# Loading V in 8 KB runs, eight heads at a time, in a cross-covariance attention kernel

One Trainium2 chip, one core. The metric is the device time of one execution in microseconds (us), median of several runs. The span of a profiled run is the part of it from the first to the last instruction. A run is called slow when it takes over 1.5% longer than the fastest run of the same kernel, else fast. Medians below count all runs; ratios, and every comparison of two kernels, use fast runs alone.

## The reference

Per head (8 x 12 heads, 512 rows n, 64 columns d), all in fp32:

```python
Q_norm = Q / norm(Q, over n);  K_norm = K / norm(K, over n)
attn = softmax(Q_norm^T K_norm, over the last axis)      # 64 x 64
out  = V attn                                            # 512 x 64
```

## The kernel before

Heads go in 24 units of four. A unit of Q, K or V is 512 KB on 128 partitions: 32 partitions per head, 16 rows (4 KB) in each. Gram matrices are taken from bf16 casts of Q and K; V is cast to bf16, transposed by TensorE into one bank of PSUM, and copied from there (evicted) by ScalarE into vt, whose slices are the weights of the last matmul. What the change and the argument touch:

```python
def load_v(u):
    vf[u] = vp.tile([128, R * D], F32, name="vf")                 # R = 16, D = 64
    nc.sync.dma_start(out=vf[u], in_=Vf[u])

def cast_v(u):                                                    # half ScalarE, half VectorE
    w = vb[u] = vbp.tile([128, R // 2, 2 * D], BF16, name="vb")
    for half, copy in ((slice(0, TP), nc.scalar.copy), (slice(TP, None), nc.vector.tensor_copy)):
        copy(w[:, half], vf[u].rearrange("p (t d) -> p t d", d=2 * D)[:, half])

def vtrans(u):
    ps = ps_v.tile([128, R // 2, 128], BF16, name="vps")
    for t in range(R // 2):
        nc.tensor.transpose(ps[:, t, :], vb[u][:, t, :], identb)
    w = vt[u] = vtp.tile([128, TP, 128, 2], BF16, name="vt")
    nc.scalar.copy(w.rearrange("p t c a -> p a t c"),             # L148, "the eviction"
                   ps.rearrange("p (a t) c -> p a t c", a=2))

def outs(u, copies=(nc.scalar.copy, nc.scalar.copy)):             # ... cut
    nc.tensor.matmul(po[...], vt[u][:, t, NV * h:NV * (h + 1), :].rearrange("p c a -> p (c a)"), ...)
    copies[g](s[:, g], po)

for s in range(U):                                                # ... cut
    on(load_qk, s + LOAD_AHEAD)
    while nv < min(U, n1 + 4):                                    # n1: units done by this step
        load_v(nv); nv += 1
    # stores, then cast_v, cast_q(s+1), norms, grams(s), ..., outs, vtrans
# closing phase: the last units' V by fp32 transposes (vtrans_f32), without a cast
```

In vt the two values with the same column c lie side by side (a), so consecutive c are 4 bytes apart. The eviction runs along c: it writes bf16 at a step of 4 bytes. The weights need (c a) at one even step, and the order of a in c decides the order of output rows, so that each partition stores 2 KB in one run.

Of the kernel before, what the change touches and what calls it, by code (L numbers as in the profile page):

```python
# [8 lines left out]
F32 = mybir.dt.float32  # L9
BF16 = mybir.dt.bfloat16  # L10
# [4 lines left out]
D = 64  # L15
HU = 4
NV = 32
R = 16
SV = 2
MV = 64  # L20
TP = 4
# [3 lines left out]
def kernel(  # L25
# [7 lines left out]
    nc = tc.nc  # L33
    B, H, N, _ = Q.shape
    assert N == NV * R and Q.shape[3] == D
    U = B * H // HU

    Qf, Kf, Vf = (x.rearrange("b h n d -> (b h n d)").rearrange("(u p f) -> u p f", p=128, f=R * D) for x in (Q, K, V))
    Of = out.rearrange("b h n d -> (b h n d)").rearrange("(u s p f) -> u p s f", s=SV, p=128, f=TP * 2 * D)

    ctx.enter_context(tc.manual_schedule())

    const = ctx.enter_context(tc.tile_pool(name="const", bufs=1))
    qp = ctx.enter_context(tc.tile_pool(name="qp", bufs=5))
    vp = ctx.enter_context(tc.tile_pool(name="vp", bufs=6))
    vbp = ctx.enter_context(tc.tile_pool(name="vbp", bufs=4))
    qkp = ctx.enter_context(tc.tile_pool(name="qkp", bufs=4))
    vtp = ctx.enter_context(tc.tile_pool(name="vtp", bufs=3))
    sop = ctx.enter_context(tc.tile_pool(name="sop", bufs=10))
# [2 lines left out]
    ps_v = ctx.enter_context(tc.tile_pool(name="ps_v", bufs=1, space=bass.MemoryType.PSUM))  # L52
# [5 lines left out]
    def outs_by(s):  # L58

        return max(0, (s - 2) * 9 // 10)  # L60


    qf, kf, vf, vb, qkb, nsq, rq, kqs, sl, ex, vt, so, kq = ({} for _ in range(13))

    def load_qk(u):
        qf[u] = qp.tile([128, R, D], F32, name="qf")
        kf[u] = qp.tile([128, R, D], F32, name="kf")
        nc.sync.dma_start(out=qf[u].rearrange("p t d -> p (t d)"), in_=Qf[u])
        nc.sync.dma_start(out=kf[u].rearrange("p t d -> p (t d)"), in_=Kf[u])

    def load_v(u):
        vf[u] = vp.tile([128, R * D], F32, name="vf")
        nc.sync.dma_start(out=vf[u], in_=Vf[u])

    def store(u, g=slice(0, SV)):
        nc.sync.dma_start(out=Of[u][:, g], in_=so[u][:, g].rearrange("p s t d -> p s (t d)"))

    def cast_q(u):
        qkb[u] = qkp.tile([128, R, 2 * D], BF16, name="qkb")
        nc.vector.tensor_copy(qkb[u][:, :, 0:D], qf[u])  # L80
# [1 line left out]
    def cast_k(u):  # L82
        nc.vector.tensor_copy(qkb[u][:, :, D:], kf[u])  # L83

    def cast_v(u):
        w = vb[u] = vbp.tile([128, R // 2, 2 * D], BF16, name="vb")
        for half, copy in ((slice(0, TP), nc.scalar.copy), (slice(TP, None), nc.vector.tensor_copy)):
            copy(w[:, half], vf[u].rearrange("p (t d) -> p t d", d=2 * D)[:, half])  # L88

    def grams(u):  # L90

# [29 lines left out]
    def logits(u):  # L121
        for h in range(HU):
            nc.tensor.transpose(lg[:, h, :], kqs[u][D:, h, :], ident[D:, D:])  # L123

    def scale_q(u):
        s = sl[u] = small.tile([D, HU, D], F32, name="sl")
        nc.vector.tensor_tensor(out=s, in0=lg, in1=rq[u][0:D, :, None].to_broadcast([D, HU, D]), op=ALU.mult)  # L127

    def exps(u):
        e = ex[u] = small.tile([D, HU, D], F32, name="ex")  # L130
        nc.scalar.activation(e, sl[u], AF.Exp)  # L131

    def normalise(u):
        s = small.tile([D, HU], F32, name="esum")
        nc.vector.reduce_sum(out=s, in_=ex[u], axis=AX.X)  # L135
        ri = small.tile([D, HU], F32, name="rinv")
        nc.vector.reciprocal(ri, s)
        a = abuf[u % len(abuf)]
        nc.vector.tensor_tensor(out=a[0:D, :, 0, :], in0=ex[u], in1=ri[:, :, None].to_broadcast([D, HU, D]), op=ALU.mult)  # L139

    def vtrans(u):

        ps = ps_v.tile([128, R // 2, 128], BF16, name="vps")
        for t in range(R // 2):
            nc.tensor.transpose(ps[:, t, :], vb[u][:, t, :], identb)  # L145

        w = vt[u] = vtp.tile([128, TP, 128, 2], BF16, name="vt")
        nc.scalar.copy(w.rearrange("p t c a -> p a t c"), ps.rearrange("p (a t) c -> p a t c", a=2))  # L148

    def vtrans_f32(u):  # L150

        w = vt[u] = vtp.tile([128, TP, 128, 2], BF16, name="vt")
        for i in range(2):
            half = slice(i * TP // 2, (i + 1) * TP // 2)
            ps = ps_t.tile([128, TP // 2, 128, 2], F32, name="vps32")
            for t in range(TP // 2):
                for a in range(2):
                    c = (a * TP + i * TP // 2 + t) * 2 * D
                    nc.tensor.transpose(ps[:, t, :, a], vf[u][:, c:c + 2 * D], ident)  # L159
            both[i](w[:, half], ps)  # L160

    def doubled(u):

        a = abuf[u % len(abuf)]
        nc.tensor.matmul(dup[D:], identb[0:D, 0:D], a[0:D, :, 0, :], tile_position=(0, D))  # L165
        nc.scalar.copy(a[D:, :, 1, :], dup[D:])  # L166

    def outs(u, copies=(nc.scalar.copy, nc.scalar.copy)):
        s = so[u] = sop.tile([128, SV, TP, 2 * D], F32, name="so")
        a = abuf[u % len(abuf)]  # L170
        for g in range(SV):
            po = ps_o.tile([128, TP, 2 * D], F32, name="po")
            for t in range(TP):
                for x in range(2):
                    h = 2 * g + x
                    nc.tensor.matmul(  # L176
                        po[MV * x:MV * (x + 1), t, :], vt[u][:, t, NV * h:NV * (h + 1), :].rearrange("p c a -> p (c a)"),
                        a[:, h].rearrange("p a d -> p (a d)"), tile_position=(0, MV * x),
                    )
            copies[g](s[:, g], po)  # L180
# [11 lines left out]
    ident = const.tile([128, 128], F32, name="ident")  # L192
    make_identity(nc, ident)
    identb = const.tile([128, 128], BF16, name="identb")
# [4 lines left out]
    for i in range(12):  # L199
        a = const.tile([128, HU, 2, D], BF16, name=f"ab{i}")  # L200
# [3 lines left out]
    def on(f, u):  # L204
        if 0 <= u < U:
            f(u)

    on(cast_q, 0)
    on(cast_k, 0)
    on(load_v, 0)  # L210
    on(load_v, 1)
    nv, nst, nt = 2, 0, 0
    for s in range(U):
        n0, n1 = outs_by(s - 1), outs_by(s)
        on(load_qk, s + LOAD_AHEAD)
        while nv < min(U, n1 + 4):
            load_v(nv)
            nv += 1
        while nst < n1 - 3:
            store(nst)  # L220
            nst += 1
        new = range(nt, n1 + 1) if s >= 1 else ()
        for v in new:
            cast_v(v)
        on(cast_q, s + 1)
        on(normalise, s - 2)
        on(grams, s)
        on(norms, s)
        on(keep_kq, s)
        on(scale_k, s)  # L230
        on(logits, s - 1)
        on(scale_q, s - 1)
        on(exps, s - 1)
        on(cast_k, s + 1)
        for v in range(n0, n1):
            outs(v)
        on(doubled, s - 2)
        for v in new:
            vtrans(v)
            nt = v + 1  # L240
# [3 lines left out]
    ps_t = ctx.enter_context(tc.tile_pool(name="ps_t", bufs=4, space=bass.MemoryType.PSUM))  # L244
    both = (nc.scalar.copy, nc.vector.tensor_copy)

    for i, u in enumerate(range(n1, U)):
        on(load_v, u + 4)
        store(u - 3)
        if i == 0:  # L250
            normalise(last - 1)
        if i == 2:
            scale_q(last)
            exps(last)
        if i == 3:
            normalise(last)
        on(vtrans_f32, u + 1)
        if i == 1:
            doubled(last - 1)
        if i == 3:  # L260
            doubled(last)
        outs(u, both)
        if i == 1:
            logits(last)
    for u in range(U - 3, last):
        store(u)
    for g in range(SV):
        store(last, slice(g, g + 1))
# [29 lines left out]
```

## Time and profile before

| | before |
|---|---|
| time, median of 3 runs | 132.05 us (131.41 to 132.57) |
| span of the profiled run | 129.3 us |
| busy: DMA engines (dynamic queue) | 98.1% |
| busy: VectorE, ScalarE, TensorE, GpSimd | 76%, 69%, 66%, 52% |
| eviction of vt, L148 | 19 x 1303 ns |
| ScalarE, cast of V | 19 x 619 ns |

How to read it: the DMA engines are the one resource near 100%; the prediction below shows the lines (columns of the timeline: start, duration, engine, line, operation, out<-in, count). These are ScalarE's instructions for one unit, from the timeline of the kernel before (columns: start, duration, engine, line, operation, out<-in, count):

```profile
82.40 1.31 ACT L148 COPY vt<-vps 128x1024 bf16<-128x1024 bf16 x1
83.56 0.63 ACT L88 CAST vb<-vf 128x512 bf16<-128x512 f32 x1
84.41 0.37 ACT L100 COPY kq<-gram 64x256 f32<-64x256 f32 x1 [0.22 <-DVE nsq L107]
84.80 0.42 ACT L131 ACTIVATE ex<-sl 64x256 f32<-64x256 f32 x1
85.24 1.07 ACT L180 COPY so<-po 128x512 f32<-128x512 f32 x2
86.34 0.37 ACT L166 CAST ab<-lgdup 64x256 bf16<-64x256 f32 x1
86.73 1.30 ACT L148 COPY vt<-vps 128x1024 bf16<-128x1024 bf16 x1
```

From one eviction to the next it is 4.33 us here, against 5.06 us of transfers per unit (three loads and a store at the pace of the loop).

### The profile page before, as it was taken

To read this page: it belongs to the slowest core of one execution; us is meant where nothing else is said; L and a number is where in the kernel's file an instruction comes from. 1 tells how busy PE (TensorE), PEld (TensorE's weight loads), DVE (VectorE), ACT (ScalarE), POOL (GpSimd) and SP (SyncE) were. 2 spreads that over 40 slices of the span, in tenths; PEclk is the share of its full clock that TensorE was granted. 3 is DMA by queue.
4 is the path that set the end of the run, shared out by engine and by line. 5 is a ranking of instruction groups with operands and counts; after the bars stand their busy time and mean duration, and the time that the engine had idled before them with its cause. 6 is when DMAs were issued, how large, how long until landed. Compare 5 with 4: busy or idle time off the path is not lost.

```text
span 129.3 us, 5436 instructions
## 1 busy us (share of the span) xinstructions
PE 85.7 (66%) x2232; PEld 65.9 (51%) x2232; DVE 98.3 (76%) x366; ACT 88.7 (69%) x158; POOL 67.6 (52%) x68
## 2 busy tenths in 40 slices
PE   0034878689667976829975776674997567697700
PEld 0033666557455754617854564452875455575500
DVE  0776787987996799839799998695699768698610
ACT  3003342548998899985795799996979997976700
POOL 7924567773785377525387768375075356500000
PEclk9999999999998699995599999997579999999995
DMA  4999999999999999999999999999999999999991
GB/s 137 402 416 418 414 403 406 412 404 402 416 403 406 416 408 412 412 408 414 404 413 411 421 406 416 409 412 411 412 411 406 416 404 413 409 411 390 348 376 68
DMA packets 16936, 50.67 MB, mean 392 GB/s; under 512 B 1552, under 2 KB 1552, under 8 KB 16912
## 3 DMA queue, kind: packets, MB, share of 16 engines
q1 hardware_dynamic: 16912, 50.34, 98.1%
q8 instruction: 17, 0.28, 0.8%
q14 instruction: 7, 0.06, 0.1%
HBM read 37.75 MB, written 12.58 MB: 389 GB/s over the span
## 4 chain that ended last, share of the span: by engine, by line
PE 25%; DMA 22%; ACT 19%; DVE 11%; issue 10%; POOL 6%; SPq 1%; ACTq 0%; POOLq 0%; DVEq 0%
DMA qf<-in_Q_dram 22%; PE gram L95 8%; ACT vt L148 7%; PE po L176 6%; ACT so L180 6%; DVE scr L107 5%; POOL rq L112 5%; PE vps L145 4%; PE vps L159 3%; ACT kq L100 3%; ACT ab L166 2%; PE lgdup L123 2%; ACT ex L131 2%; PE lgdup L165 2%; POOL kqs L117 1%
## 5 line engine op out<-in xcount | busy, mean ns | idle before, releaser
L112 POOL TENSOR_TENSOR rq<-nsq,mhalf 128x4 f32<-128x4 f32 x24 | 45.9, 1913 | 42.5 <-DVE nsq L107 31.7
L95 PE MATMUL gram<-qkb 32*128 32x128 bf16 x1536 | 34.1, 248 | 18.3 <-DVE qkb L83 11.4
L95 PEld LDWEIGHTS <-qkb 32*128 32x128 bf16 x1536 | 28.2, 110 | 25.1 <-DVE qkb L83 15.0
L107 DVE CUSTOM_DVE_ANT_0 scr<-gram,ident 128x128 f32<-128x128 f32 x96 | 22.0, 283 | 12.1 <-PE gram L95 11.9
L100 ACT COPY kq<-gram 64x256 f32<-64x256 f32 x24 | 8.8, 367 | 26.6 <-DVE nsq L107 26.3
L148 ACT COPY vt<-vps 128x1024 bf16<-128x1024 bf16 x19 | 24.8, 1303 | 0.5
L80 DVE CAST qkb<-qf 128x1024 bf16<-128x1024 f32 x24 | 19.3, 804 | 6.0 <-DMA qf<-in_Q_dram 6.0
L180 ACT COPY so<-po 128x512 f32<-128x512 f32 x42 | 22.8, 588 | 1.2 <-PE po L176 0.5
L176 PE MATMUL po<-ab,vt 128*64 128x128 bf16 x384 | 18.0, 241 | 5.6 <-ACT vt L148 4.4
L176 PEld LDWEIGHTS <-vt 128*64 128x64 bf16 x384 | 13.4, 121 | 12.1 <-ACT vt L148 5.9
L123 PE MATMUL lgdup<-ident,kqs 64*64 64x64 f32 x96 | 11.6, 250 | 7.1 <-POOL kqs L117 5.2
L83 DVE CAST qkb<-kf 128x1024 bf16<-128x1024 f32 x24 | 16.2, 676 | 0.0
L117 POOL TENSOR_TENSOR kqs<-kq,rq 64x256 f32<-64x256 f32 x24 | 15.1, 628 | 1.9
L145 PE MATMUL vps<-identb,vb 128*128 128x128 bf16 x152 | 14.1, 246 | 0.0
L145 PEld LDWEIGHTS <-vb 128*128 128x128 bf16 x152 | 10.3, 110 | 5.2 <-ACT kq L100 3.1
L88 ACT CAST vb<-vf 128x512 bf16<-128x512 f32 x19 | 11.8, 619 | 0.5 <-DMA vf<-in_V_dram 0.4
L123 PEld LDWEIGHTS lgdup<-ident,kqs 64*64 64x64 f32 x96 | 7.1, 122 | 9.6 <-POOL kqs L117 8.2
L131 ACT ACTIVATE ex<-sl 64x256 f32<-64x256 f32 x24 | 10.0, 417 | 2.5 <-DVE sl L127 2.0
L127 DVE TENSOR_TENSOR sl<-lgdup,rq 64x256 f32<-64x256 f32 x24 | 9.9, 411 | 2.3 <-PE lgdup L123 2.3
L165 PE MATMUL lgdup<-ab,identb 64*64 64x256 bf16 x24 | 7.6, 318 | 5.5 <-DVE sl L127 4.4
L139 DVE TENSOR_TENSOR ab<-ex,rinv 64x256 bf16<-64x256 f32 x24 | 10.3, 431 | 0.8
L135 DVE TENSOR_REDUCE esum<-ex 64x4 f32<-64x256 f32 x24 | 9.7, 402 | 1.0 <-ACT ex L131 1.0
(20 smaller groups left out, 59.5 us busy)
## 6 DMA issues: line engine op xcount, KB each, us to landing
qf<-in_Q_dram SPq DMA_DIRECT2D x24, 512.0 KB, 10.2
kf<-in_K_dram SPq DMA_DIRECT2D x24, 512.0 KB, 10.2
vf<-in_V_dram SPq DMA_DIRECT2D x24, 512.0 KB, 10.2
out_dram<-so SPq DMA_DIRECT2D x23, 512.0 KB, 10.0
out_dram<-so SPq DMA_DIRECT2D x2, 256.0 KB, 5.0
```

The costliest lines, as they stand in the source:

```text
L80: nc.vector.tensor_copy(qkb[u][:, :, 0:D], qf[u])
L83: nc.vector.tensor_copy(qkb[u][:, :, D:], kf[u])
L95: nc.tensor.matmul(gbuf[:, h, 0:2 * D], x, x, start=(t == 0), stop=(t == R - 1), tile_position=(NV * h, 0))
L100: nc.scalar.copy(kq[u][D:], gbuf[D:, :, 0:D])
L107: nc.vector.tensor_tensor_reduce(out=scr, in0=gbuf[:, h, 0:2 * D], in1=ident, scale=1.0, scalar=1e-20, op0=ALU.mult, op1=ALU.add, accum_ou ...
L112: nc.gpsimd.tensor_tensor(out=r, in0=n2, in1=mhalf, op=ALU.pow)
L117: nc.gpsimd.tensor_tensor(out=kk[D:], in0=kq[u][D:], in1=rq[u][D:, :, None].to_broadcast([D, HU, D]), op=ALU.mult,)
L123: nc.tensor.transpose(lg[:, h, :], kqs[u][D:, h, :], ident[D:, D:])
L145: nc.tensor.transpose(ps[:, t, :], vb[u][:, t, :], identb)
L148: nc.scalar.copy(w.rearrange("p t c a -> p a t c"), ps.rearrange("p (a t) c -> p a t c", a=2))
L176: nc.tensor.matmul(po[MV * x:MV * (x + 1), t, :], vt[u][:, t, NV * h:NV * (h + 1), :].rearrange("p c a -> p (c a)"), a[:, h].rearrange("p ...
L180: copies[g](s[:, g], po)
```

## The change

Intent: the transfers bound the kernel, so make them cheaper. V is loaded in 12 pieces of 1 MB, eight heads side by side, 16 partitions per head, and each partition reads 32 rows, one run of 8 KB. A piece serves two units. Each partition now holds four values per column c (a of 4), which the casts, transposes and evictions follow in halves. The core of the diff:

```diff
-    Qf, Kf, Vf = (x.rearrange(...)... for x in (Q, K, V))
+    Vf = V.rearrange("b h n d -> (b h n d)").rearrange("(w p f) -> w p f", p=128, f=2 * R * D)
-    vp  bufs=6, vbp bufs=4
+    vp  bufs=4, vbp bufs=3
@@ cast_v: half of the unit each for ScalarE and VectorE, as before
-            copy(w[:, half], vf[u].rearrange("p (t d) -> p t d", d=2 * D)[:, half])
+        x = vf[w].rearrange("p (a t d) -> p a t d", a=A, d=2 * D)
+            copy(vb[w][:, :, t], x[:, :, t])
@@ vtrans
-        w = vt[u] = vtp.tile([128, TP, 128, 2], BF16, name="vt")
-        nc.scalar.copy(w.rearrange("p t c a -> p a t c"), ps.rearrange("p (a t) c -> p a t c", a=2))
+            vt[w] = vtp.tile([128, TP, 128, A], BF16, name="vt")                     # A = 4
+        nc.scalar.copy(vt[w][:, 2 * i:2 * i + 2].rearrange("p t c a -> p a t c"), ps)
@@ the loop
-        while nv < min(U, n1 + 4):
+        while nv < min(U, n1 + 5) // 2:
-        new = range(nt, n1 + 1) if s >= 1 else ()
+        new = range(nt, n1 + 2) if s >= 1 else ()
@@ closing phase
-        on(vtrans_f32, u + 1)
+        on(vtrans_f32, u + 2)
```

With a of 4, consecutive c in vt are 8 bytes apart: the eviction's write step doubles.

More of the change, by code (lines that the diff above doesn't have):

```diff
@@ L18 @@
 R = 16
+HV = 8
+NP = 16
+A = 4
 SV = 2
@@ L36 @@
     U = B * H // HU
-    Qf, Kf, Vf = (x.rearrange("b h n d -> (b h n d)").rearrange("(u p f) -> u p f", p=128, f=R * D) for x in (Q, K, V))
+    Qf, Kf = (x.rearrange("b h n d -> (b h n d)").rearrange("(u p f) -> u p f", p=128, f=R * D) for x in (Q, K))
+    Vf = V.rearrange("b h n d -> (b h n d)").rearrange("(w p f) -> w p f", p=128, f=2 * R * D)
     Of = out.rearrange("b h n d -> (b h n d)").rearrange("(u s p f) -> u p s f", s=SV, p=128, f=TP * 2 * D)
@@ L44 @@
     qp = ctx.enter_context(tc.tile_pool(name="qp", bufs=5))
-    vp = ctx.enter_context(tc.tile_pool(name="vp", bufs=6))
-    vbp = ctx.enter_context(tc.tile_pool(name="vbp", bufs=4))
+    vp = ctx.enter_context(tc.tile_pool(name="vp", bufs=4))
+    vbp = ctx.enter_context(tc.tile_pool(name="vbp", bufs=3))
     qkp = ctx.enter_context(tc.tile_pool(name="qkp", bufs=4))
@@ L69, in load_qk, with load_v @@
         nc.sync.dma_start(out=kf[u].rearrange("p t d -> p (t d)"), in_=Kf[u])
-    def load_v(u):
-        vf[u] = vp.tile([128, R * D], F32, name="vf")
-        nc.sync.dma_start(out=vf[u], in_=Vf[u])
+    def load_v(w):
+        vf[w] = vp.tile([128, 2 * R * D], F32, name="vf")
+        nc.sync.dma_start(out=vf[w], in_=Vf[w])
     def store(u, g=slice(0, SV)):
@@ L83, in cast_k, with cast_v @@
         nc.vector.tensor_copy(qkb[u][:, :, D:], kf[u])
-    def cast_v(u):
-        w = vb[u] = vbp.tile([128, R // 2, 2 * D], BF16, name="vb")
-        for half, copy in ((slice(0, TP), nc.scalar.copy), (slice(TP, None), nc.vector.tensor_copy)):
-            copy(w[:, half], vf[u].rearrange("p (t d) -> p t d", d=2 * D)[:, half])
+    def cast_v(v):
+        w, i = divmod(v, 2)
+        if i == 0:
+            vb[w] = vbp.tile([128, A, TP, 2 * D], BF16, name="vb")
+        x = vf[w].rearrange("p (a t d) -> p a t d", a=A, d=2 * D)
+        for t, copy in ((2 * i, nc.scalar.copy), (2 * i + 1, nc.vector.tensor_copy)):
+            copy(vb[w][:, :, t], x[:, :, t])
     def grams(u):
@@ L139, in normalise, with vtrans, vtrans_f32 @@
         nc.vector.tensor_tensor(out=a[0:D, :, 0, :], in0=ex[u], in1=ri[:, :, None].to_broadcast([D, HU, D]), op=ALU.mult)
-    def vtrans(u):
-        ps = ps_v.tile([128, R // 2, 128], BF16, name="vps")
-        for t in range(R // 2):
-            nc.tensor.transpose(ps[:, t, :], vb[u][:, t, :], identb)
-        w = vt[u] = vtp.tile([128, TP, 128, 2], BF16, name="vt")
-        nc.scalar.copy(w.rearrange("p t c a -> p a t c"), ps.rearrange("p (a t) c -> p a t c", a=2))
-    def vtrans_f32(u):
-        w = vt[u] = vtp.tile([128, TP, 128, 2], BF16, name="vt")
-        for i in range(2):
-            half = slice(i * TP // 2, (i + 1) * TP // 2)
-            ps = ps_t.tile([128, TP // 2, 128, 2], F32, name="vps32")
-            for t in range(TP // 2):
-                for a in range(2):
-                    c = (a * TP + i * TP // 2 + t) * 2 * D
-                    nc.tensor.transpose(ps[:, t, :, a], vf[u][:, c:c + 2 * D], ident)
-            both[i](w[:, half], ps)
+    def vtrans(v):
+        w, i = divmod(v, 2)
+        ps = ps_v.tile([128, A, 2, 128], BF16, name="vps")
+        for t in range(2):
+            for a in range(A):
+                nc.tensor.transpose(ps[:, a, t, :], vb[w][:, a, 2 * i + t, :], identb)
+        if i == 0:
+            vt[w] = vtp.tile([128, TP, 128, A], BF16, name="vt")
+        nc.scalar.copy(vt[w][:, 2 * i:2 * i + 2].rearrange("p t c a -> p a t c"), ps)
+    def vtrans_f32(v):
+        w, i = divmod(v, 2)
+        if i == 0:
+            vt[w] = vtp.tile([128, TP, 128, A], BF16, name="vt")
+        for t in range(2 * i, 2 * i + 2):
+            ps = ps_t.tile([128, 128, A], F32, name="vps32")
+            for a in range(A):
+                c = (a * TP + t) * 2 * D
+                nc.tensor.transpose(ps[:, :, a], vf[w][:, c:c + 2 * D], ident)
+            both[t % 2](vt[w][:, t], ps)
     def doubled(u):
@@ L170, in outs @@
         a = abuf[u % len(abuf)]
+        v = vt[u // 2][:, :, u % 2 * 64:(u % 2 + 1) * 64]
         for g in range(SV):
@@ L176, in outs @@
                     nc.tensor.matmul(
-                        po[MV * x:MV * (x + 1), t, :], vt[u][:, t, NV * h:NV * (h + 1), :].rearrange("p c a -> p (c a)"),
+                        po[MV * x:MV * (x + 1), t, :], v[:, t, NP * h:NP * (h + 1), :].rearrange("p c a -> p (c a)"),
                         a[:, h].rearrange("p a d -> p (a d)"), tile_position=(0, MV * x),
@@ L209 @@
     on(cast_k, 0)
-    on(load_v, 0)
-    on(load_v, 1)
-    nv, nst, nt = 2, 0, 0
+    load_v(0)
+    nv, nst, nt = 1, 0, 0
     for s in range(U):
@@ L247 @@
     for i, u in enumerate(range(n1, U)):
-        on(load_v, u + 4)
+        while nv < min(U, u + 6) // 2:
+            load_v(nv)
+            nv += 1
         store(u - 3)
```

## The prediction

> **What bounds the kernel now.** I read the page's 40 slices first, then the DMA part, then the waits of the DMA queue, then the end of the timeline. The slices and the DMA lines:
>
> ```profile
> DMA  4999999999999999999999999999999999999991
> GB/s 137 402 416 418 414 403 406 412 404 402 416 403 406 416 408 412 412 408 414 404 413 411 421 406 416 409 412 411 412 411 406 416 404 413 409 411 390 348 376 68
> DMA packets 16936, 50.67 MB, mean 392 GB/s; under 512 B 1552, under 2 KB 1552, under 8 KB 16912
> ...
> q1 hardware_dynamic: 16912, 50.34, 98.1%
> ...
> vf<-in_V_dram SPq DMA_DIRECT2D x24, 512.0 KB, 10.2
> ```
>
> The DMA engines are 90% or more busy in every slice but the first and the last, and the rate is flat at 400 to 420 GB/s, both while only loads run (slices 2 to 10) and while a quarter of the traffic is stores. VectorE is at 76%, ScalarE at 69%, TensorE at 66%. The waits of the DMA queue agree:
>
> ```profile
> SPq L69 <- DMA kf<-in_K_dram: 11.8, 13, 1.3
> SPq L76 <- DVE so L180: 10.0, 5, 4.0
> SPq L76 <- DMA out_dram<-so: 10.0, 11, 0.9
> SPq L68 <- DMA qf<-in_Q_dram: 9.8, 13, 0.9
> SPq L73 <- DMA vf<-in_V_dram: 9.5, 11, 1.0
> ```
>
> Almost every issue waits about 1 us for an earlier transfer to land: eight are in flight, and the trace's landings come 1.27 us apart, which is 512 KB at 413 GB/s. The one other large entry, stores that wait for so, is the end, where SyncE is out of loads. Even there the engines have a backlog: in the landing records the last nine stores land at 119.5, 120.8, 122.0, 123.2, 124.5, 125.8, 127.1, 127.7 and 128.4 us, although the last was issued at 123.3. So **the DMA engines bound the span from 2 us to 128.4 us**. The last result:
>
> ```profile
> 121.39 0.68 DVE L180 COPY so<-po 128x512 f32<-128x512 f32 x1
> 122.57 0.69 DVE L180 COPY so<-po 128x512 f32<-128x512 f32 x1 [0.50 <-PE po L176]
> ```
>
> It is ready at 123.3. A 256 KB store on an empty queue would need, by my estimate, some 2.6 us (0.64 us of data, and about 2 us of latency: the first load took 3.4 us for 512 KB). So computing could end about 2.4 us later before it set the end. That reserve matters below.
>
> I also grouped the trace's DMA packets by size (median duration on one of 16 engines):
>
> ```
> 4 B (completion)   1553 packets    9 ns
> 2048 B (stores)    6144 packets   84 ns
> 4096 B (loads)     9216 packets  159 ns
> 8192 B (instruction loads) 13    314 ns, 5th percentile 308
> ```
>
> 84 to 159 is 75 ns per 2048 B, so a packet costs 9 ns plus 27.3 B/ns. 16 engines at 4096 B per 159 ns are 412 GB/s: just the plateau of the slices. The plateau is the packets' own rate.
>
> **What the Trainium skill says.** "DMA: Bandwidth & Descriptors", section "Why small descriptors are slow (HBM only)", names a fixed cost of about 3 cycles per packet. The trace agrees that there is one, 9 ns by the line through its sizes. The same page, "Rules for kernel authors", asks for at least 1 MiB per DMA for most bandwidth. With eight in flight this trace holds its packet-limited rate at 512 KB, so I expect nothing from that alone. "Perfetto Trace Analysis", section "DMA Optimizations", says that going from 2 KB to 4 or 8 KB "can dramatically improve throughput". Here it can't: 2 KB packets move 24.4 B/ns, 4 KB 25.8, 8 KB would move 26.5. "SBUF — State Buffer", section "Door 1: The DMA port swizzle", says that strided access is free while at least two accesses fall in a 16-byte line; no run so far shows it for this stride.
>
> **The change part by part.**
>
> 1. *Packets of V.* 12.58 MB in 3072 packets of 4 KB become 1536 of 8 KB, if the hardware does not cut them. Two of 159 ns are 318, one of 8 KB is 9 + 300 = 309 (the 13 seen: 308 and up). 1536 x 9 ns / 16 engines = **0.86 us less**. Twelve transfers fewer are 192 completion packets fewer, 192 x 9 / 16 = **0.11 us less**. Sum 0.97 us, all on the path while the engines have work: 0.75% of 129.3.
>
> 2. *Issue.* 24 issues of V at 0.33 us become 12. SyncE waits anyway: nothing.
>
> 3. *Casts, transposes, evictions.* Comparing the instruction streams: still 24 casts of each kind except that unit 19 moves from the closing phase into the loop (20 instead of 19 units go by bf16 casts, 4 instead of 5 by f32 transposes). The casts have the same 512 elements (619 ns ScalarE, 418 VectorE), now in four runs. The eviction of vt (L148, 1303 ns) writes with a step of 8 bytes instead of 4, by the page still two to a line: I take it as unchanged. ScalarE's work per unit is 619 + 367 + 417 + 2 x 588 + 368 + 1303 = 4.25 us against 5.06 us of DMA time for four transfers, so it needs +0.8 us before ScalarE becomes the bound. The f32 transposes of the end write PSUM with a step of 16 bytes instead of 8 (273 ns each); they are 32 instead of 40, so the closing phase loses about 1.1 us of TensorE and 0.6 of each eviction engine.
>
> 4. *When V is there.* This is the part that moves. Before, V of a unit was issued three steps ahead of its cast. Now a pair is issued two steps ahead, behind the Q and K of the step which casts it, and lands as one piece: 1.27 (K) + 2.5 us after that step's Q. In the landing and cast records the casts of Q lag behind the landing by 5 to 6 us in steps 8 to 13 (no wait for V), but only by 1.3 us in steps 17 to 21. There cast_v, which stands first in VectorE's queue, must wait. I put the landings of before against the new order of bytes, less the saving: the pairs for steps 17, 19 and 21 land at 82.4, 92.4 and 102.9, against VectorE casts at 80.4, 90.4 and 99.0:
>
> ```profile
> 98.97 0.41 DVE L88 CAST vb<-vf 128x512 bf16<-128x512 f32 x1
> 99.37 0.69 DVE L80 CAST qkb<-qf 128x1024 bf16<-128x1024 f32 x1
> ...
> 103.50 0.43 DVE L88 CAST vb<-vf 128x512 bf16<-128x512 f32 x1
> 104.94 0.77 DVE L80 CAST qkb<-qf 128x1024 bf16<-128x1024 f32 x1 [1.01 <-DMA qf<-in_Q_dram]
> ```
>
> The last of these waits delays VectorE by 3.9 us. One step takes it about 4.2, so the next cast of Q comes at 107.3 instead of 104.9: 2.4 us late. The DMA does not feel it in the loop (eight transfers in flight, five buffers of Q, stores issued three steps after their outs). The closing phase starts 2.4 us late and is 1.3 us shorter (one f32 unit less): the last so comes at about 124.4. With 2.6 us of store that is 127.0, and the packet-limited landing of the last store is 128.36 - 0.97 = 127.4. The stores of units 18 to 22 must each be issued about 3.5 us ahead of their place; 20 and 21 will be some 0.3 and 1.2 us late for it, and such bubbles are not made good at the end. I charge **0.4 us** for it.
>
> Sum: 132.05 - 0.97 + 0.4 = **131.5 us**.
>
> **The rivals.**
>
> *A: all of the saving shows, or more.* The wait for V is soaked up and the end stays DMA-bound: 131.1. For more than 1 us, 8 KB runs would have to be served faster than 27.3 B/ns. Loads at 4 KB and mixed traffic with 2 KB stores run at the same 410 GB/s, which speaks against a strong effect of run length. 129.5 at best.
>
> *B: the wait for V takes the place of what is removed.* If the delay of 2.4 us isn't shortened by the lost f32 unit, the last so comes at 125.7 or later, and the end is 128.5 to 129.5: 132.2 to 133.2. For it: VectorE reaches 4.4 us in some steps, and throttled TensorE slices (PEclk 5) slow a step. Against: 2.4 us of reserve.
>
> *C: vt's eviction becomes the bound.* L148 takes 1303 ns for 1024 elements, while the f32 eviction takes 588 for 512, so something in bf16 or in the step already costs about 0.2 us. If twice the step adds 0.8 us or more, ScalarE has over 5.06 us per unit, the lag no longer shrinks and the end falls 4 us behind: 135. About 6%.
>
> *D: nothing, because 8 KB descriptors are cut into 4 KB packets.* Then only 0.11 us is saved, and step 4 still costs: 132.3.
>
> **Range and chances.** A, the middle case and B span 131.1 to 133.2, and the three timed runs of before alone span 131.4 to 132.6. So 130.0 to 133.2. Faster by 2% needs 129.4, more than twice what the packets can give: 5%. Slower by 2% needs 134.7, which only C reaches: 7%. Within 2%: 88%.
>
> **What will show it.** Step 1: packets on the dynamic queue fall from 16912 to about 15184, those of V take about 309 ns, and the loads' plateau rises to about 416 GB/s. Step 3: L148's successor stays at 1.3 us, 20 of them. Step 4: a new wait of VectorE for vf in the waits, in steps 17, 19 and 21, up to 4 us; the last cast of Q near 107; the last so at about 124.4; lower GB/s in the last slices. I am wrong if the packets stay at 4 KB, if vt's eviction grows past 2 us, or if the closing stores leave the engines idle for more than 1 us.

## The result

| | before | after |
|---|---|---|
| median, 6 runs each | 131.74 us | 146.68 us |
| ratio of fast runs | | 1.111 (95%: 1.104 to 1.118), slower |
| span of the profiled run | 129.3 | 145.1 |

A ratio here is the mean time of one kernel's fast runs over that of the other's fast runs of the same rounds, so not quite the ratio of the medians. One of the six runs of after was slow (148.44) and is left out of it.

The page of after: 40 equal slices of the span (the first two lines in tenths of busy time) and the packets:

```profile
ACT  3003665439999999999999599999999999984640
...
DMA  4999999999999999999999999999998824303665
GB/s 166 367 429 409 417 409 413 418 402 413 410 405 421 407 418 422 412 417 402 414 413 420 408 417 416 414 413 421 410 395 299 325 81 149 116 33 145 250 251 225
...
q1 hardware_dynamic: 15184, 50.34, 87.3%
```

ScalarE is at 90% or more from slice 10 to slice 35, but for slice 23. The DMA engines keep their plateau up to slice 29, then run dry: the last Q and K land by 106.8 us, the last V by 115.6, and the stores wait for results. The packets did what was hoped: 15184 instead of 16912, and the packet records show 1536 of 8192 bytes at a median of 309 ns, for 318 as two of 4 KB.

The eviction in before and in after (busy us and mean ns follow the bar; then idle time just before, with what ended it), and below it the chain's shares by engine, again of before and of after. The chain is the work that ended last, followed back from the end, each step to what released it:

```profile
L148 ACT COPY vt<-vps 128x1024 bf16<-128x1024 bf16 x19 | 24.8, 1303 | 0.5
L159 ACT COPY vt<-vps 128x1024 bf16<-128x1024 bf16 x20 | 48.9, 2445 | 1.6 <-PE vps L155 1.1
```

```profile
PE 25%; DMA 22%; ACT 19%; DVE 11%; issue 10%; POOL 6%; SPq 1%; ACTq 0%; POOLq 0%; DVEq 0%
ACT 42%; PE 25%; issue 12%; DMA 7%; DVE 7%; POOL 2%; SPq 2%; ACTq 0%; POOLq 0%
```

The eviction takes **2445 ns instead of 1303**, 20 times: 48.9 us of ScalarE instead of 24.8. In the chain of before ScalarE had 19%, here it has 42%. Its timeline for one unit of after:

```profile
94.05 2.43 ACT L159 COPY vt<-vps 128x1024 bf16<-128x1024 bf16 x1
96.22 0.69 ACT L96 CAST vb<-vf 128x512 bf16<-128x512 f32 x1
96.93 0.37 ACT L108 COPY kq<-gram 64x256 f32<-64x256 f32 x1
97.32 0.42 ACT L139 ACTIVATE ex<-sl 64x256 f32<-64x256 f32 x1
97.76 1.07 ACT L192 COPY so<-po 128x512 f32<-128x512 f32 x2
98.86 0.37 ACT L177 CAST ab<-lgdup 64x256 bf16<-64x256 f32 x1
99.25 2.46 ACT L159 COPY vt<-vps 128x1024 bf16<-128x1024 bf16 x1
```

No gap at all, and 5.20 us from eviction to eviction instead of 4.33: more than the 5.06 us of transfers. Among the waits (us in total, times, longest) other engines now stand behind ScalarE:

```profile
DVE esum L143 <- ACT ex L139: 14.3, 16, 2.2
...
PEld L188 <- ACT vt L159: 10.9, 8, 1.9
```

Where the 15.8 us of span went: in the records of issues and landings, the last store is issued at 141.1 us instead of 123.3, that is 17.8 us later. Before, it then landed 5.1 us after its issue, behind a backlog; after, the queue is empty and it takes 2.9. 17.8 - 2.2 = 15.6.

The excess of 0.14 us per unit over the transfers would not make 15 us. What was lost is the reserve. In before, computing starts late and then catches up: VectorE's cast of Q runs up to 6.5 us behind the landing of its data in the middle of the run, and the last one starts at once. In after the period of 5.2 us leaves nothing to catch up with, and the last cast of Q is 12.1 us behind (in the runs below: 9.9 in e1, 6.4 in e8, where ScalarE has less to do, and 1.6 in e3, with the eviction repaired). The last cast of K is 13.8 us later than in before (121.58 instead of 107.78); from there to the issue of the last store it takes 19.5 us instead of 15.5, which is the other 4.0.

The order of waits changed too. From the fifth pair on VectorE casts V 7 to 18 us after it has landed, and Q 10 to 13 us after. The wait for V that the prediction feared does not exist here, but for the first piece: everything computes so late that V is long there.

### The profile page after: what moved, and what is told of

The parts are those of the page before. It is cut to its first block, busy times and chain, and to the rows that moved or that the text cites. A ratio compares the mean times of both kernels' runs of the same rounds, so it can differ in the third digit from the quotient of the medians.

```text
span 145.1 us, 5388 instructions
## 1 busy us (share of the span) xinstructions
PE 93.0 (64%) x2232; PEld 73.0 (50%) x2232; DVE 99.5 (69%) x366; ACT 111.9 (77%) x159; POOL 72.4 (50%) x68
## 3 DMA queue, kind: packets, MB, share of 16 engines
q1 hardware_dynamic: 15184, 50.34, 87.3%
## 4 chain that ended last, share of the span: by engine, by line
ACT 42%; PE 25%; issue 12%; DMA 7%; DVE 7%; POOL 2%; SPq 2%; ACTq 0%; POOLq 0%
ACT vt L159 20%; PE gram L103 10%; ACT so L192 8%; DMA vf<-in_V_dram 7%; PE po L188 6%; ACT ab L177 4%; PE vps L155 4%; ACT vb L96 3%; ACT kq L108 3%; ACT ex L139 3%; DVE scr L115 3%; PE vps L170 3%; POOL rq L120 2%; PE lgdup L176 2%; DVE so L192 1%
## 5 line engine op out<-in xcount | busy, mean ns | idle before, releaser
L120 POOL TENSOR_TENSOR rq<-nsq,mhalf 128x4 f32<-128x4 f32 x24 | 51.2, 2133 | 52.3 <-DVE nsq L115 46.2
L159 ACT COPY vt<-vps 128x1024 bf16<-128x1024 bf16 x20 | 48.9, 2445 | 1.6 <-PE vps L155 1.1
L103 PE MATMUL gram<-qkb 32*128 32x128 bf16 x1536 | 37.8, 272 | 12.2 <-DVE qkb L87 10.7
L103 PEld LDWEIGHTS <-qkb 32*128 32x128 bf16 x1536 | 32.5, 122 | 18.0 <-DVE qkb L87 14.1
L115 DVE CUSTOM_DVE_ANT_0 scr<-gram,ident 128x128 f32<-128x128 f32 x96 | 22.1, 286 | 15.2 <-PE gram L103 14.9
L188 PE MATMUL po<-ab,vt 128*64 128x128 bf16 x384 | 19.6, 246 | 10.5 <-ACT vt L159 9.6
L155 PE MATMUL vps<-identb,vb 128*128 128x128 bf16 x160 | 16.4, 264 | 13.8 <-ACT vb L96 10.0
L192 ACT COPY so<-po 128x512 f32<-128x512 f32 x42 | 22.8, 588 | 2.1 <-PE po L188 1.6
L188 PEld LDWEIGHTS <-vt 128*64 128x64 bf16 x384 | 13.9, 124 | 15.8 <-ACT vt L159 10.9
L155 PEld LDWEIGHTS <-vb 128*128 128x128 bf16 x160 | 12.2, 118 | 17.7 <-ACT vb L96 12.2
L96 ACT CAST vb<-vf 128x512 bf16<-128x512 f32 x20 | 13.5, 678 | 1.9 <-DMA vf<-in_V_dram 1.9
L131 PEld LDWEIGHTS lgdup<-ident,kqs 64*64 64x64 f32 x96 | 7.7, 131 | 9.9 <-issue 6.6
L177 ACT CAST ab<-lgdup 64x256 bf16<-64x256 f32 x24 | 8.8, 367 | 2.1 <-PE lgdup L176 1.5
```

Of the source, the lines that this page charges most:

```text
L96: copy(vb[w][:, :, t], x[:, :, t])
L103: nc.tensor.matmul(gbuf[:, h, 0:2 * D], x, x, start=(t == 0), stop=(t == R - 1), tile_position=(NV * h, 0))
L115: nc.vector.tensor_tensor_reduce(out=scr, in0=gbuf[:, h, 0:2 * D], in1=ident, scale=1.0, scalar=1e-20, op0=ALU.mult, op1=ALU.add, accum_ou ...
L120: nc.gpsimd.tensor_tensor(out=r, in0=n2, in1=mhalf, op=ALU.pow)
L131: nc.tensor.transpose(lg[:, h, :], kqs[u][D:, h, :], ident[D:, D:])
L155: nc.tensor.transpose(ps[:, a, t, :], vb[w][:, a, 2 * i + t, :], identb)
```

## The experiments

The theory, S: the eviction's write step, 8 bytes instead of 4, doubles its time and makes ScalarE the bound. The rivals: T, it is the shape (four long runs, or reading PSUM as bf16), not the step; W, it is V's late arrival in pairs; and, once S held, what became of the saved 0.97 us.

### m1: the copies by themselves

A kernel that only times copies, three of each kind, profiled once:

```python
d = tile([128, 1024, step], BF16)[:, :, 0]      # write step of 2 x step bytes
copy(d, ps)                                      # ps: 1024 bf16 of PSUM; copy: ScalarE or VectorE
copy(d4.rearrange("p t c a -> p a t c"), ...)    # the eviction's form, a of 2 and of 4: "step"
copy(d4, ps.rearrange("p (a t) c -> p t c a"))   # the same copy, loops turned round: "turned"
```

> A kernel that only measures (its output is V copied, wrong on purpose): ScalarE and VectorE copies of 1024 bf16 or 512 fp32 elements per partition, whose writes to SBUF step by 2, 4, 8 or 16 bytes, and the eviction's own forms of before and after, also with the loops turned round (contiguous writes, stepped reads of PSUM). Theory S (the step of the write is what costs): ScalarE's copy of 1024 bf16 takes about 1.0 us at a step of 2 bytes, 1.3 at 4, 2.4 at 8, whatever the source, and the turned form of four takes 1.0 to 1.3. Rival T (it is the shape: four long runs, or PSUM read as bf16): flat copies take the same at 4 and at 8 bytes, about 1.3, and only the form of after takes 2.4. VectorE: no strong view; the f32 evictions of the closing phase took it 0.69 us for 512.

Measured, in one look; the forms as the timeline shows them (three copies to a line; the first line of each kind is a of 2, the second a of 4):

```profile
33.47 4.28 ACT L77 COPY s_evict_a_step<-pb 128x1024 bf16<-128x1024 bf16 x3
37.61 3.10 ACT L80 COPY s_evict_a_turned<-pb 128x1024 bf16<-128x1024 bf16 x3
40.60 7.33 ACT L77 COPY s_evict_a_step<-pb 128x1024 bf16<-128x1024 bf16 x3
47.68 3.20 ACT L80 COPY s_evict_a_turned<-pb 128x1024 bf16<-128x1024 bf16 x3
...
85.45 7.32 DVE L77 COPY v_evict_a_step<-pb 128x1024 bf16<-128x1024 bf16 x3
92.57 3.76 DVE L80 COPY v_evict_a_turned<-pb 128x1024 bf16<-128x1024 bf16 x3
```

And the flat copies, the last of three, ns, by write step:

| copy | 2 bytes | 4 bytes | 8 bytes | 16 bytes |
|---|---|---|---|---|
| ScalarE, 1024 bf16 from PSUM | 1012 | 1291 | 2421 | 4681 |
| ScalarE, 1024 bf16 from SBUF | 1045 | 1327 | 2461 | |
| ScalarE, 512 fp32 from PSUM to bf16 | 585 | 726 | 1290 | |
| ScalarE, 512 fp32 from PSUM to fp32 | | 586 | 614 | 1067 |
| VectorE, 1024 bf16 from PSUM | 691 | 1293 | 2431 | 4691 |
| VectorE, 1024 bf16 from SBUF | 427 | 742 | 1302 | |

T falls: flat copies have the same times as the eviction's forms (1291 and 2420 in the records), and so does a copy from SBUF by ScalarE. What counts is the step of the write. ScalarE's bf16 copies grow by 4.4 ns for every further 16 bytes over which the writes are spread: from a step of 4 to 8 bytes, where 4 KB more are 256 times 16 bytes, (2421 - 1291) / 256, and from 8 to 16, (4681 - 2421) / 512. For fp32 from 8 to 16 bytes it is (1067 - 614) / 256 = 1.8 ns. Why bf16 pays more than twice as much these runs don't say, nor whether lines of 16 bytes are the reason: no step over 16 bytes was run. Stepped reads of PSUM, on the other hand, cost ScalarE nothing: the turned form reads at 512 or 1024 bytes and takes 1012 ns, like the flat copy at 2 bytes. VectorE's last turned copies take 1225 ns, against 691 flat, so there such reads did cost. With stepped writes VectorE pays the same as ScalarE from PSUM, so handing it the eviction as it is would not help.

### e1: the step alone, in the kernel before

```diff
-  w = vt[u] = vtp.tile([128, TP, 128, 2], BF16, name="vt")
+  w = vt[u] = vtp.tile([128, TP, 128, 2, 2], BF16, name="vt")[:, :, :, :, 0]
```

The same edit stands in vtrans_f32, so that the evictions of the closing phase step as well (4 bytes, from fp32).

> The kernel before with one thing changed: every second element of vt is left empty, so that the eviction writes at a step of 8 bytes and the weights are read at 4; V is loaded as before, in 4 KB runs and 512 KB pieces. Theory S (the eviction's write step makes ScalarE the bound): L148 goes from 1.30 to about 2.4 us, ScalarE runs without gaps at 5.2 us per unit, the time is 143 to 148 us. Rival W (what costs is that V comes late, in pairs behind Q and K): L148 may lengthen, but the time stays within 132 to 135 us. Weight loads at 4 bytes may lengthen; if they go from 110 to over 200 ns this run no longer tells the two apart.

Measured: correct, **143.24 us** (141.57 to 144.44, one of four runs slow), ratio 1.086 (1.079 to 1.093). The three fast runs average 142.7, just under the range. Its groups:

```profile
L148 ACT COPY vt<-vps 128x1024 bf16<-128x1024 bf16 x19 | 46.4, 2443 | 0.5
...
L176 PEld LDWEIGHTS <-vt 128*64 128x64 bf16 x384 | 15.4, 136 | 23.3 <-ACT vt L148 20.6
```

The eviction takes 2443 ns; the weight loads, read at 4 bytes, 136 ns on average for 121 (with a lower TensorE clock in this profile, 0.747), far from the 200 at which the run would have told nothing. With V loaded exactly as before, most of the loss is there, 11.3 of 14.6 us between the means of fast runs: W falls as its main cause. The 3 us less than in after may come from one eviction fewer in the loop and from V in single units; that was not tested.

### e3: the step taken away, V as in after

```diff
-  nc.scalar.copy(vt[w][:, 2 * i:2 * i + 2].rearrange("p t c a -> p a t c"), ps)
+  nc.scalar.copy(vt[w][:, 2 * i:2 * i + 2], ps.rearrange("p a t c -> p t c a"))
```

> The kernel after with the loops of the eviction turned round: it writes vt contiguously and reads the bank of PSUM at a step of 512 bytes. V's loads are those of after. Theory S: if reads may step, L159 takes 1.0 to 1.4 us and the time is 130.5 to 132 us (the 0.97 us of packets saved, less up to 0.5). If a step hurts reads of PSUM as well, it takes over 2 us and the time stays above 142. Rival W: above 140 us, however short L159 is.

Measured: correct, 132.01 us (131.05 to 132.71, and a slow run of 135.21), ratio 1.002 (0.996 to 1.008). Repeated in a later job as e9:

> e3_after_contig once more, to stand on one chip beside e10: 131.5 to 132.3 us, within 0.7% of before.

e9: 132.40 us (131.90 to 133.78, and a slow run of 135.22), ratio 1.007 (1.002 to 1.013). The fast runs average 131.69 in e3, inside the range, and 132.55 in e9, slightly beyond it. In e3 the eviction takes 1012 ns, 20 times. One turned line gives back all of the 15 us: the theory holds from this side as well. It also lays bare the rest: the packets are saved, yet nothing is gained. The slices of e3's page, and VectorE's waits for V in e3 and in e9:

```profile
GB/s 160 329 414 425 426 402 405 408 424 395 421 413 399 433 402 410 423 405 410 419 407 410 412 424 413 407 424 409 415 415 415 409 412 414 413 308 283 285 273 207
```

```profile
DVE vb L96 <- DMA vf<-in_V_dram: 4.1, 2, 2.1
DVE vb L96 <- DMA vf<-in_V_dram: 8.2, 4, 2.5
```

Here is the wait for V of the prediction's fourth part. About 2 us of each total are the very first piece. Beyond that e3 has one wait, of 2.0 us at 103.72, and e9 three, at 83.53, 93.51 and 103.53, in the very steps that the prediction named (17, 19 and 21). In the last five slices of e3 the DMA engines move 207 to 308 GB/s instead of over 400. The last cast of Q starts at 107.75 us, 1.56 after its data; in the kernel before at 104.94, at once. From unit 18 on each store lands 2.8 to 3.5 us after its issue: the end follows the computing, no longer the transfers.

This profile is of the slowest fast run of e3 (132.71; the other two took 131.05 and 131.32), and V is not the only thing that differs: just there the granted TensorE clock was 0.5, from 106.0 to 112.9 us. Two stretches of it (us of the span; then its length, the busy times of PE, PEld, DVE, ACT and POOL, the granted clock, the DMA share and GB/s):

```profile
106.00:110.00 4.00, 3.05 (x73) 2.40 (x72) 3.35 (x13) 3.25 (x7) 3.21 (x2) 0.50 1.03 411
110.00:114.00 4.00, 4.00 (x99) 3.09 (x95) 2.86 (x13) 3.22 (x7) 2.27 (x2) 0.64 1.05 419
```

In the profile of before both stretches have the full clock. So how much of the late end is V and how much the clock, this profile does not settle; e5 and e10 below do so in part.

### e4: another way to take the step away

```diff
-  nc.tensor.transpose(ps[:, a, t, :], vb[w][:, a, 2 * i + t, :], identb)     # 8 of them, one copy of 1024
+  nc.tensor.matmul(ps[:, :, a], vb[w][:, a, t, :], identb)                   # 4 of them, fp32, in vt's order
+  nc.scalar.copy(vt[w][:, t], ps)                                            # 512 contiguous, twice
```

> The kernel after with the bf16 transposes replaced by bf16 matmuls against the identity, which write fp32 to PSUM already in the order of vt (a step of 16 bytes), a quarter of the pair at a time; ScalarE then copies 512 fp32 contiguous elements twice per unit. Theory S: 2 x 0.59 = 1.18 us instead of 2.45 per unit, ScalarE has 4.2 us per unit again, and the time is 130.5 to 133 us; a bank that TensorE and ScalarE use in turns may cost some waits of TensorE, within the 5.06 us of a unit. Rival W: above 140 us.

A clear miss: **177.44 us**, ratio 1.348. ScalarE's part came true (its line below), but the two halves share the one bank that is free:

```profile
L157 PE MATMUL vps<-identb,vb 128*128 128x128 bf16 x160 | 35.3, 417 | 33.4 <-ACT vt L158 32.3
...
L158 ACT CAST vt<-vps 128x512 bf16<-128x512 f32 x40 | 23.4, 586 | 23.1 <-PE vps L157 22.7
```

TensorE waits 32.3 us for the bank to be evicted, in its own queue, in front of the next Gram matrices. ScalarE is idle half of the span. The run says nothing against S, but a fix must not move the wait to TensorE; and its matmuls, which write at 16 bytes, took 417 ns on average for 246 of the transposes before (at a mean clock of 0.778 for 0.922).

### e7: V earlier, eviction left slow

```diff
-  while nv < min(U, n1 + 5) // 2:
+  while nv < min(U, n1 + 5 + (n1 > 0)) // 2:
```

> The kernel after, eviction untouched (2.45 us), with each pair of V issued one step earlier from the fourth step on. If ScalarE's eviction is the whole bound, V's arrival has nothing to do with it here (VectorE casts Q 12 us after it lands), and the time stays at 145.5 to 147.5 us. If V's lateness has a part in the loss, it falls by 1 us or more.

Measured: 148.10 us (146.95 to 148.52, one slow run of 149.21), ratio 1.123. No gain; the fast runs average 147.7, a little above the range. These runs show no part of V's arrival in the loss of after.

### e8: ScalarE relieved elsewhere

```diff
-  outs(v)
+  outs(v, (nc.scalar.copy, nc.vector.tensor_copy))      # in the loop
```

> The kernel after, eviction untouched, but one of the two copies of so per unit goes to VectorE instead of ScalarE. ScalarE's work per unit falls by 0.59 us, from about 5.45 to 4.86, under the 5.06 us that the transfers of a unit take; VectorE's rises by 0.69 to about 4.9. If ScalarE's load is what lengthens after, the time falls to 133 to 138 us. If it is the order of things around the slow eviction (TensorE waiting for vt), it falls by less than 4 us.

Measured: fast runs of 138.12 and 137.39 us, two slow ones (139.55, in which the profile fell, and 140.57); ratio of the fast 1.047 (1.039 to 1.055). With the eviction as slow as in after (2.45 us in the timeline), 0.59 us less of ScalarE per unit takes off over 8 us: ScalarE's load is the bound of after. The fast runs lie at the upper end of what was expected, one of them just above it; the timeline's evictions start 4.74 us apart, near the 4.86 worked out, but VectorE now has hardly a gap either (80% of the span). Even so the last cast of Q is 6.4 us behind its landing, where in before the lag is gone. What else is in the 6 us over the kernel before was not taken apart.

### m2 and m3: the transfers by themselves

No computing: Q, K and V loaded, zeros stored, V in 4 KB (m2) or 8 KB runs (m3).

```python
for u in range(24):                       # m3: V every other u, [128, 2048] instead of [128, 1024]
    load Q[u], K[u], V[u];  store out[u - 4] from one tile
```

> The transfers alone (the output is zeros, wrong on purpose): Q, K and V loaded as in the kernel before, V in 24 pieces of 512 KB and 4 KB runs, 24 stores of 2 KB runs, no computing. By the packets: 9216 x 159 + 6144 x 84 + 1536 x 9 ns over 16 engines is 124.7 us, with start and end about 128 to 129 us measured. If it takes 130 or more, the kernel before had nothing to lose in its computing at all.

> The same with V in 12 pieces of 1 MB and 8 KB runs. By the packets 0.97 us less than with 4 KB runs (1536 x 9 ns for the runs and 192 x 9 ns for the completions, over 16 engines), 0.6 to 1.3 allowed. If 8 KB runs brought nothing on the chip, the difference would be under 0.3.

Measured: m2 128.63 us (128.23 to 129.26), m3 127.95 us (127.42 to 128.87), both six runs in the same job. The difference of the medians is **0.68 us**, inside the 0.6 to 1.3 expected, but the runs of the two overlap, so its sign is likely and its size is not settled. And m2 tells that all computing in the kernel before costs about 3 us of 131.46 (ratio of m2 to it: 0.977, 95%: 0.973 to 0.982).

### e5 and e10: both repaired

e3, with e7's earlier V.

> The kernel after with the turned eviction (1.01 us) and, from the fourth step on, each pair of V issued one step earlier, as far ahead of its cast as before. If the wait for V is what eats the saved 0.97 us, the waits of VectorE for vf fall from 4.1 us to under 1, the last cast of Q comes at 106 to 106.5 instead of 107.75, the stores of the end keep the DMA engines over 90% busy one or two slices longer, and the time is 0.5 to 1.2 us under e3's (132.0), that is 130.8 to 131.5 and 0 to 0.7% under the kernel before. If the wait is only a sign and the end is set by something else (Q of the last step lands 1.3 us later because more of V is ahead of it), the time stays at e3's.

Measured: 130.87 us (130.47 to 132.26, and a slow run of 133.91), ratio to before 0.9955 (0.990 to 1.001). Its slices and VectorE's wait for V:

```profile
GB/s 157 359 395 429 426 402 409 405 429 392 420 411 418 404 411 421 405 410 418 414 403 412 425 404 414 416 420 409 418 418 409 403 422 414 410 386 364 343 396 80
```

```profile
DVE vb L96 <- DMA vf<-in_V_dram: 1.6, 1, 1.6
```

VectorE waits 1.6 us for V instead of 4.1 (what is left is the very first piece, so that the wait in the loop is gone), the last cast of Q starts at 105.81, at once after its landing, and the DMA engines stay busy nearly to the end. That is about as expected. e3 ran on another chip; by the ratios to before the gain over e3 is 0.7%, or 0.9 us, and the two intervals overlap. Beside e9, on one chip:

> e5_contig_early_v once more beside e9: 130.5 to 131.2 us, 0.6 to 1.2 us under e9, and 0.2 to 0.8% under the kernel before.

Measured: 131.52 us (130.80 to 132.46), above the range; the mean of fast runs is 0.96 under e9's, but the ratio to before is 1.000 (0.994 to 1.006). So the earlier V looks worth about 0.9 us in both jobs, each time with overlapping intervals: likely, not settled. A gain over the kernel before is not shown: 0.45% in e5, within its interval, and none in e10. The runs of e5 and e10 fall in two clusters, near 130.8 and near 132.3; those of before in the job of e10 do as well (seven at 131.05 to 131.38, four at 132.11 to 132.49). The profile of e5 is of the first (130.89), that of e10 of the second (132.46), and they differ in the TensorE clock as the closing phase starts. One stretch of e10 and then of e5, in the columns of e3's above:

```profile
110.00:114.00 4.00, 3.20 (x76) 2.41 (x73) 1.43 (x10) 2.41 (x5) 1.16 (x2) 0.51 1.02 405
110.00:114.00 4.00, 2.91 (x73) 2.17 (x60) 2.92 (x15) 3.76 (x8) 2.47 (x4) 1.00 1.03 407
```

At 0.51 of the clock the last Gram matrices, on which the last units hang, take 1.89 us instead of 1.07, and e10's unit 18 is stored at 117.8 instead of 115.1. The last five slices of e10 then look like e3's (313, 286, 288, 274 and 208 GB/s), though V is early and no cast in the loop waits for it. So idle DMA engines at the end are no sure sign of a late V. That the clock makes the two clusters is argued from one profile each, not shown.

### e6: the turned eviction in the kernel before

```diff
-  nc.scalar.copy(w.rearrange("p t c a -> p a t c"), ps.rearrange("p (a t) c -> p a t c", a=2))
+  nc.scalar.copy(w, ps.rearrange("p (a t) c -> p t c a", a=2))
```

> The kernel before with only the loops of the eviction turned round, so that it writes contiguously. L148 goes from 1.30 to 1.01 us, 19 times, 5.5 us less of ScalarE. The DMA engines bound this kernel, so the time stays within 0.5% of before; a gain of over 1% would mean that ScalarE did set the pace somewhere.

Measured: 131.58 us (130.95 to 131.97), ratio 0.999 (0.995 to 1.003), eviction 1012 ns. 5.6 us less of ScalarE and no change: there it set no part of the time that these runs can resolve. No version here beats the kernel before clearly.

## Why the prediction was wrong

- **The bound of before (DMA): right.** m2 and e6 confirm it: without any computing it still takes 128.63 us, and with 5.6 us less of ScalarE the same time.
- **Part 1, the packets: right** in count and duration (15184, 309 ns); the plateau rose less than to 416 (slices 3 to 29 average 414 GB/s for 411). The 0.97 us that this is worth showed as 0.68 in the transfers alone, within their scatter.
- **Part 2, the issue: nothing**, as said; no run contradicts it.
- **Part 3: this step failed.** "The eviction of vt (L148, 1303 ns) writes with a step of 8 bytes instead of 4, by the page still two to a line: I take it as unchanged." It went to 2445 ns. That is 1.14 us more per unit, above the reserve of 0.8 worked out one sentence later, and 22.8 us of ScalarE in all. What stood in its place is rival C, given 6% and 135 us: ScalarE became the bound and the lag no longer shrank. C was right as a mechanism and sized too small: it took the point at which ScalarE becomes the bound (+0.8 us) and an end 4 us behind; at +1.14 the last result came 17.8 us later. The prediction's own sign of being wrong, an eviction past 2 us, came true.
- The warning was in the trace of before. The Trainium skill, "ScalarE: Activation LUTs", section "What ACT_TABLE_LOAD costs", gives 186 ns + 0.833 ns per element for an ACTIVATE with immediate scale and bias: by this, as an estimate, 1039 ns for 1024 elements and 613 for 512. The copies of 512 took 588, which about agrees; L148 took 1303. Those 264 ns too much were the price of the 4-byte step, already visible: contiguous writes take 1012 (m1). The prediction saw the excess (under C, as about 0.2 us), let the sentence about 16-byte lines overrule it, and put a low chance on a cost that had left its mark.
- **Part 4, V's arrival: right in kind, hidden in after.** In after itself no wait of it appears, since ScalarE makes everything later than V. With the eviction repaired it is there: the waits of e9 in steps 17, 19 and 21 (1.7 to 2.5 us, for up to 4 predicted), the last cast of Q at 107.75 in e3 and 107.57 in e9 (predicted near 107). Mis-sized was what follows. The closing phase was to start 2.4 us late and be 1.3 us shorter for one fp32 unit less; in e3 the last cast of K came 3.6 us late, and from there to the issue of the last store it took 15.4 us, for 15.5 in before (14.8 in e9, 15.2 in e5, 18.2 in e10). So the last result came at 126.7 in e3, not at 124.4, and the whole saving was lost, not 0.4 of it. A part of this can be the halved clock, which the prediction could not know. (Its reading that casts of Q lag by 5 to 6 us in steps 8 to 13 is rough: the records have 4.3 to 6.5.)
- **Rivals A and B.** They could be met only with the repaired eviction. With V late the fast runs average 131.7 (e3) and 132.6 (e9), below and inside B's 132.2 to 133.2; with V early 131.0 (e5) and 131.6 (e10), around A's 131.1. D fell: 8 KB runs are one packet each.

## What to carry to other kernels

A change of layout for one engine sets the access step of the next one: before a transfer-bound kernel gets longer runs, work out the write step of every copy that follows, and if a copy already takes longer than its element count says, expect that excess to grow with the step (here from 0.3 to 1.4 us over a contiguous copy). On ScalarE, turn the loops so that the writes are contiguous and the reads of PSUM take the step. An engine off the path still has a reserve that lets late work catch up; count what a change takes from it. And a saving on the bounding resource only shows if the work behind it still keeps pace to the end: here pieces twice as large had to be issued a step earlier for the waits to go.

## What the Trainium skill lacked or had wrong

- "SBUF — State Buffer", section "Door 1: The DMA port swizzle (why `[64,N]` ≈ `[32,N]`)": at least two accesses to a 16-byte line are needed for full bandwidth, and one can stride for free over 4 fp32 or 8 bf16 elements. For bf16 writes this is not so: ScalarE takes 1012, 1291, 2421 and 4681 ns for 1024 elements at steps of 2, 4, 8 and 16 bytes, with four, two and one element to a line at the last three. For fp32, where the page calls 4 elements free, a step of two about holds and one of four does not: 586, 614 and 1067 ns for 512 elements at 4, 8 and 16 bytes.
- "ScalarE: Activation LUTs", section "What ACT_TABLE_LOAD costs": the formula gives, as an estimate, 1039 ns for 1024 elements and about fits contiguous writes (1012 to 1045 ns). The page says nothing of the write step, which here makes up to 4681.
- "Perfetto Trace Analysis", section "DMA Optimizations": batching small transfers, "e.g., 2KB → 4KB or 8KB", is said to "dramatically improve throughput". It gives no sizes for runs inside large transfers, where little is left: from 4 KB to 8 KB runs, for a quarter of the traffic, the transfers alone fell by 0.68 of 128.63 us; a packet of 8192 bytes takes 309 ns, two of 4096 take 318.
